# Add and GELU on one core: one 64 KB-row load for the first half of y, another split of the additions, and turns between VectorE and GpSimd

## The chip, the cores and the metric

The kernel runs on one core of a Trainium2 chip. The metric is device time in microseconds (us), the median of several runs; the core also leaves one profiled execution, whose records are read below. The engines that matter are VectorE (DVE in the profile), ScalarE (ACT), GpSimd (POOL) and SyncE (SP), which does no arithmetic and only issues the transfers between the device memory and the on-chip memory (SBUF). TensorE (PE) has no work here.

## The reference

```python
x, y: float32, 1024 x 4096
z = x + y
out = 0.5 * z * (1 + tanh(sqrt(2 / pi) * (z + 0.044715 * z**3)))
```

This is an addition followed by the tanh form of GELU. Each element is read once from x and once from y and written once: 2 x 16.78 MB in, 16.78 MB out.

## The kernel before, in words

Each of the three arrays is seen as 128 partitions x 32768 columns of float32. One SBUF tile `z` holds all 32768 columns: x is loaded into it, y is added in place, the result replaces the sum in place, and the stores read it. The arithmetic goes by 16 chunks of 2048 columns, numbered 0 to 15. For each chunk c there are four steps:

- `add(c)`, line 149: z + y into z, on VectorE for the chunks in the table `by_dve` (line 109), otherwise on GpSimd. Both inputs are in SBUF.
- `mag(c)`, line 154: ScalarE writes |z| into a PSUM buffer `w`. There are two such buffers (`PS = 2`), so `mag(c)` waits for `end(c - 2)` as well as for `add(c)`.
- `gelu(c)`, line 157: ScalarE replaces w by gelu(-w). With a = |z| that is gelu(-a).
- `end(c)`, line 166: VectorE writes max(z, 0) + w into z. One input is in SBUF, the other in PSUM. (For both signs of z, max(z, 0) + gelu(-|z|) is gelu(z).)

All transfers are issued by SP, in one fixed order, on one hardware queue: x0 (columns 0 to 16383, a row of 64 KB in each partition), y0 and y1 (8192 columns each, rows of 32 KB), x1 (columns 16384 to 32767, rows of 64 KB), y2, y3 (8192 columns each), and then the stores s0 (chunks 0 to 7), s1 (chunks 8 to 12) and s2 (chunks 13 to 15). SP takes them strictly in turn: while it waits for one to be allowed, all that follow wait too. The y loads go round two SBUF buffers of 8192 columns (`pool_y`, `bufs=2`, line 115). So y2 needs adds 0 to 3 to be done, since they read the buffer that it overwrites, and y3 needs adds 4 to 7. `begin_early` (line 9) moves the first two loads, which wait for nothing, ahead of the start barrier. `wait_late` (line 23) lets the closing work of the other engines run while the last store is under way.

Each engine's order is written out in lines 173 to 181. The value of an entry of `by_dve` says ahead of which `end` VectorE does that add: `{0: 0, 2: 0, 4: 2, 6: 4, 8: 8, 12: 10}` means adds 0 and 2, end 0, end 1, add 4, end 2, end 3, add 6, end 4, and so on. GpSimd does its ten adds in the order of the chunks, ScalarE `mag` and `gelu` by turns. The table `needs` (line 183) only fixes the order in which the program is written down; the semaphore waits come from which bytes of which tile each instruction reads and writes. One more wait is put in by hand (lines 137 to 143): s0, and with it everything behind it on SP, waits for the first half of `end(8)`, which is why `end(FIRST)` with `FIRST = 8` is cut in two parts.

Of the kernel before, what the change touches and what calls it, by code (L numbers as in the profile page):

```python
# [8 lines left out]
def begin_early(nc, count):  # L9


    head, body = (b.instructions for b in nc.main_func.blocks[:2])
    SP = mybir.EngineType.SP
    moved = [i for i in body if i.engine == SP and isinstance(i, mybir.InstDMACopy)][:count]
    assert not any(i.sync_info and i.sync_info.on_wait for i in moved)
    assert all(i.regs_accessed() == ((), ()) for i in moved)
    at = next(k for k, i in enumerate(head) if i.engine == SP)
    for k, i in enumerate(moved):
        body.remove(i)
        head.insert(at + k, i)  # L20


def wait_late(nc):

    body, end = (b.instructions for b in nc.main_func.blocks[1:3])
    last = [i for i in body if isinstance(i, mybir.InstDMACopy)][-1]
    (sem,) = [u.id for u in last.sync_info.on_update]
    all_done = end[0]  # L30
    reset = next(i for i in end if isinstance(i, mybir.InstDrain) and i.is_reset_sema)
    at = end.index(reset)
    clear = end[at + 1]
    first, stop = reset.reset_range_start, reset.reset_range_stop
    assert all_done.engine == mybir.EngineType.SP and reset.engine == mybir.EngineType.Pool
    assert isinstance(clear, mybir.InstISA) and clear.engine == mybir.EngineType.Pool
    waits = all_done.sync_info.on_wait
    (its,) = [w for w in waits if w.id == sem]

    end[0] = mybir.InstDrain(  # L40
        name=all_done.name, engine=all_done.engine, debug=all_done.debug, is_reset_sema=False,
        sync_info=mybir.SyncInfo(on_wait=[w for w in waits if w.id != sem], on_update=[]),
    )
    parts = []
    for f, e in ((first, sem), (sem + 1, stop)):
        if f < e:
            nc.gpsimd.sem_clear(range(f, e))
            parts.append(nc.cur_bb.bb.instructions.pop())
    end[at + 1 : at + 2] = parts
    end.append(  # L50
        mybir.InstEventSemaphore(
            name=clear.name, engine=mybir.EngineType.Activation, debug=clear.debug,
            sync_info=mybir.SyncInfo(
                on_wait=[its],
                on_update=[
                    mybir.SyncUpdate(
                        sync_type="semaphore", id=sem, ant_name=its.ant_name,
                        update_mode="sem-sub-imm", update_value=its.wait_value,
                    )
                ],  # L60
            ),
        )
    )


@with_exitstack
def kernel(
    ctx: ExitStack,
    tc: tile.TileContext,
    x: bass.AP,  # L70
    y: bass.AP,
    out: bass.AP,
):

    nc = tc.nc
    P = nc.NUM_PARTITIONS
    fp32 = mybir.dt.float32
    act = mybir.ActivationFunctionType
    alu = mybir.AluOpType

    N, D = x.shape
    assert N % P == 0
    TOT = N // P * D  # L90
    xv, yv, ov = (a.rearrange("(p n) d -> p (n d)", p=P) for a in (x, y, out))

    YS = 8192
    CH = 2048
    PS = 2
    xloads = [16384, 16384]
    yloads = [8192, 8192, 8192, 8192]
    FIRST = 8
    stores = [16384, 10240, 6144]

    def ranges(sizes):
        ends = [sum(sizes[: i + 1]) for i in range(len(sizes))]
        assert ends[-1] == TOT
        return [(e - f, e) for e, f in zip(ends, sizes)]

    xr, yr, sr, cr = (ranges(r) for r in (xloads, yloads, stores, [CH] * (TOT // CH)))
    C = len(cr)

    by_dve = {0: 0, 2: 0, 4: 2, 6: 4, 8: 8, 12: 10}

    def over(rs, lo, hi):
        return [i for i, (a, b) in enumerate(rs) if a < hi and b > lo]

    pool_sb = ctx.enter_context(tc.tile_pool(name="xz", bufs=1))
    pool_y = ctx.enter_context(tc.tile_pool(name="y", bufs=2))
    pool_w = ctx.enter_context(
        tc.tile_pool(name="w", bufs=PS, space=bass.MemoryType.PSUM)
    )

    zt = pool_sb.tile([P, TOT], fp32, tag="z", name="z")  # L120
    yt, wt, ends = {}, {}, {}

    def load_x(i):
        a, b = xr[i]
        nc.sync.dma_start(out=zt[:, a:b], in_=xv[:, a:b])  # L125

    def load_y(i):
        a, b = yr[i]
        s, o = divmod(a, YS)
        if o == 0:  # L130
            yt[s] = pool_y.tile([P, YS], fp32, tag="y", name=f"y{s}")
        nc.sync.dma_start(out=yt[s][:, o : o + b - a], in_=yv[:, a:b])

    def store(i):
        a, b = sr[i]
        ins = nc.sync.dma_start(out=ov[:, a:b], in_=zt[:, a:b])
        if i == 0:
            tc.add_manual_dep(
                ins.ins,
                ends[FIRST].name,  # L140
                mybir.DependencyInfo(mybir.DependencyClass.Sync, mybir.DependencyReason.DATA),
                reason="the stores join the queue when the last load is nearly done",
            )

    def add(c):
        a, b = cr[c]
        s, o = divmod(a, YS)
        eng = nc.vector if c in by_dve else nc.gpsimd
        eng.tensor_add(out=zt[:, a:b], in0=zt[:, a:b], in1=yt[s][:, o : o + b - a])  # L149

    def mag(c):
        a, b = cr[c]
        wt[c] = pool_w.tile([P, CH], fp32, tag="w", name=f"w{c}")
        nc.scalar.activation(out=wt[c], in_=zt[:, a:b], func=act.Abs)  # L154

    def gelu(c):
        nc.scalar.activation(  # L157
            out=wt[c], in_=wt[c], func=act.Gelu_apprx_tanh, scale=-1.0
        )

    def end(c):
        a, b = cr[c]
        parts = 2 if c == FIRST else 1
        n = (b - a) // parts
        for o in range(0, b - a, n):
            ins = nc.vector.scalar_tensor_tensor(  # L166
                out=zt[:, a + o : a + o + n], in0=zt[:, a + o : a + o + n], scalar=0.0,
                in1=wt[c][:, o : o + n], op0=alu.max, op1=alu.add,
            )
            ends.setdefault(c, ins.ins)  # L170


    sp = []
    for i, (a, b) in enumerate(xr):
        sp += [(load_x, i)] + [(load_y, j) for j, (c, _) in enumerate(yr) if a <= c < b]
    sp += [(store, i) for i in range(len(stores))]
    pool = [(add, c) for c in range(C) if c not in by_dve]
    dve, acts = [], []
    for c in range(C):
        dve += [(add, k) for k in sorted(by_dve) if by_dve[k] == c] + [(end, c)]  # L180
        acts += [(mag, c), (gelu, c)]

    needs = {
        load_x: lambda i: [],
        load_y: lambda i: [
            (add, c) for c in over(cr, yr[i][0] - 2 * YS, yr[i][1] - 2 * YS)
        ],
        add: lambda c: [(load_x, i) for i in over(xr, *cr[c])]
        + [(load_y, i) for i in over(yr, *cr[c])],
        mag: lambda c: [(add, c)] + ([(end, c - PS)] if c >= PS else []),  # L190
        gelu: lambda c: [(mag, c)],
        end: lambda c: [(gelu, c)],
        store: lambda i: [(end, c) for c in over(cr, *sr[i])] + [(end, FIRST)],
    }
    queues = [sp, pool, acts, dve]
    done = set()
    with tc.manual_schedule():
        one = pool_sb.tile([P, 1], fp32, tag="one", name="one")
        nc.vector.memset(one, 0.0)  # L199
        nc.scalar.activation(out=one, in_=one, func=act.Gelu_apprx_tanh)  # L200
        while any(queues):
            moved = False
            for q in queues:
                while q and all(n in done for n in needs[q[0][0]](q[0][1])):
                    fn, arg = q.pop(0)
                    fn(arg)
                    done.add((fn, arg))
                    moved = True
                    if q is not sp:
                        break  # L210
            assert moved, [q[:1] for q in queues]

    ctx.close()
    tc.close()
    tc.compile()  # L215
    begin_early(nc, 2)
    wait_late(nc)
# [30 lines left out]
```

## Time and profile before

| what | us |
|---|---|
| median of 8 runs | 120.13 (120.03 to 120.29) |
| the profiled execution | 120.08 |
| its span, first to last recorded work | 118.6 |
| DMA engines busy | 98.7% of the span |
| ACT busy, DVE busy, POOL busy | 60.8, 59.8, 55.5 |
| bytes moved | 50.33 MB, 424 GB/s over the span |

The span leaves out 1.5 us around the recorded work. [...] The DMA figure is the mean over 16 DMA engines, which share each transfer: every one moves 8 of its 128 rows. A row is recorded as one packet with a start, a duration and a size. A transfer has landed when the last of the 16 has reported its share. Times in the text are counted from the span's start.

### The profile page before, as it was taken

Reading aid. Unit: us, or ns where it says so; the run is one execution under the profiler, and the core shown is the slowest. Engines: PE = TensorE matmul, PEld = TensorE weight load, DVE = VectorE, ACT = ScalarE, POOL = GpSimd, SP = SyncE. Lnnn points to the kernel's source line nnn. Section 1 sums busy time; section 2 is a strip of 40 time slices with the busy share of each in tenths; the row PEclk is TensorE's granted clock in tenths of the full one; section 3 lists DMA queues with packets and bytes.
Section 4 is the critical chain, followed back from the end, with each engine's and each line's share of the span. In section 5 each row is a group of like instructions: output and inputs, shape, how many; then the busy total and the mean of one; then the engine's idle time right before and its main releaser. Section 6 shows DMA issues by size and latency. Waiting matters only on the chain.

```text
span 118.6 us, 160 instructions
## 1 busy us (share of the span) xinstructions
DVE 59.8 (50%) x24; ACT 60.8 (51%) x34; POOL 55.5 (47%) x14
## 2 busy tenths in 40 slices
DVE  0000000000399999699994584257999457742000
ACT  5000000000057979999379705797798999940000
POOL 0000000000399999998000029999999999200000
DMA  9899888989999988988899998998899889999996
GB/s 354 354 420 641 354 354 354 497 387 464 420 409 475 531 354 354 707 354 354 354 464 420 398 486 354 531 531 354 354 597 464 354 354 442 442 442 442 390 406 265
DMA packets 1296, 50.33 MB, mean 424 GB/s; under 512 B 144, under 2 KB 144, under 8 KB 144
## 3 DMA queue, kind: packets, MB, share of 16 engines
q1 hardware_dynamic: 1296, 50.33, 98.7%
HBM read 33.55 MB, written 16.78 MB: 424 GB/s over the span
## 4 chain that ended last, share of the span: by engine, by line
DMA 48%; POOL 34%; POOLq 4%; ACT 3%; DVE 2%; issue 0%; SPq 0%; DVEq 0%
DMA y<-in_y_dram 48%; POOL z L149 34%; POOLq L215 4%; DVE z L166 2%; ACT w L154 2%; ACT w L157 2%; SPq L125 0%; POOLq L149 0%; DVEq L166 0%
## 5 line engine op out<-in xcount | busy, mean ns | idle before, releaser
L149 POOL TENSOR_TENSOR z<-z,y 128x2048 f32<-128x2048 f32 x10 | 55.3, 5566 | 45.7 <-DMA y<-in_y_dram 45.7
L154 ACT ACTIVATE w<-z 128x2048 f32<-128x2048 f32 x16 | 30.1, 1880 | 42.6 <-DVE z L149 36.1
L166 DVE SCALAR_TENSOR_TENSOR z<-z,w 128x2048 f32<-128x2048 f32 (+1 forms) x17 | 36.4, 2157 | 16.0 <-ACT w L157 16.0
L149 DVE TENSOR_TENSOR z<-z,y 128x2048 f32<-128x2048 f32 x6 | 24.0, 4008 | 30.4 <-DMA y<-in_y_dram 30.4
L157 ACT ACTIVATE w<-w 128x2048 f32<-128x2048 f32 x16 | 29.8, 1862 | 0.5
L200 ACT ACT_TABLE_LOAD x1 | 1.3, 1283 | 1.2 <-PEq L232 1.2
L199 DVE MEMSET one<- 128x1 f32 x1 | 0.1, 59 | 1.3 <-PEq L232 1.3
L200 ACT ACTIVATE one<-one 128x1 f32<-128x1 f32 x1 | 0.2, 203 | 0.0
L232 POOL MEMSET const-float32-0.0<- 128x1 f32 x1 | 0.1, 98 | 0.2 <-issue 0.2
L232 POOL MEMSET const-bfloat16-1.0<- 128x1 bf16 x1 | 0.1, 102 | 0.0
L232 POOL MEMSET const-uint8-127<- 128x1 uint8 x1 | 0.1, 102 | 0.0
L232 POOL MEMSET const-float32-1.0<- 128x1 f32 x1 | 0.1, 99 | 0.0
## 6 DMA issues: line engine op xcount, KB each, us to landing
y<-in_y_dram SPq DMA_DIRECT2D x4, 4096.0 KB, 28.2
out_dram<-z SPq DMA_DIRECT2D x1, 5120.0 KB, 14.9
out_dram<-z SPq DMA_DIRECT2D x1, 3072.0 KB, 10.9
z<-in_x_dram SPq DMA_DIRECT2D x2, 40.3
out_dram<-z SPq DMA_DIRECT2D x1, 21.6
```

The lines of the kernel that those rows point to most:

```text
L149: eng.tensor_add(out=zt[:, a:b], in0=zt[:, a:b], in1=yt[s][:, o : o + b - a])
L154: nc.scalar.activation(out=wt[c], in_=zt[:, a:b], func=act.Abs)
L157: nc.scalar.activation(out=wt[c], in_=wt[c], func=act.Gelu_apprx_tanh, scale=-1.0)
L166: ins = nc.vector.scalar_tensor_tensor(out=zt[:, a + o : a + o + n], in0=zt[:, a + o : a + o + n], scalar=0.0, in1=wt[c][:, o : o + n], op ...
L199: nc.vector.memset(one, 0.0)
L200: nc.scalar.activation(out=one, in_=one, func=act.Gelu_apprx_tanh)
L215: tc.compile()
L232: nc = _bacc.Bacc("TRN2", target_bir_lowering=False, num_devices=1)
```

## The change

The first half of y becomes one load of 16384 columns (rows of 64 KB) into one buffer `y` of that size, in place of two loads into two buffers of half the size; the SBUF taken is the same. The second half of y is still two loads of 8192 columns, y1 and y2 in the new numbering, into the first and the second half of that buffer. VectorE does adds 0, 1, 3, 5, 7, 8, 11 and 14 and GpSimd the other eight. Six of GpSimd's adds (2, 4, 6, 9, 12, 15) get a wait for the VectorE add just before them, by the table `turn`; adds 10 and 13 have none. The hand-made wait of the stores is taken out, and with it the cut of `end(8)` in two.

```diff
-    YS = 8192
+    YS = 16384
-    yloads = [8192, 8192, 8192, 8192]
-    FIRST = 8
+    yloads = [16384, 8192, 8192]
-    by_dve = {0: 0, 2: 0, 4: 2, 6: 4, 8: 8, 12: 10}
+    by_dve = {0: 0, 1: 0, 3: 1, 5: 3, 7: 5, 8: 6, 11: 9, 14: 12}
+
+    turn = {2: 1, 4: 3, 6: 5, 9: 8, 12: 11, 15: 14}
-    pool_y = ctx.enter_context(tc.tile_pool(name="y", bufs=2))
+    yt = pool_sb.tile([P, YS], fp32, tag="y", name="y")
     def load_y(i):
         a, b = yr[i]
-        s, o = divmod(a, YS)
-        if o == 0:
-            yt[s] = pool_y.tile([P, YS], fp32, tag="y", name=f"y{s}")
-        nc.sync.dma_start(out=yt[s][:, o : o + b - a], in_=yv[:, a:b])
+        o = a % YS
+        nc.sync.dma_start(out=yt[:, o : o + b - a], in_=yv[:, a:b])
     def store(i):
         a, b = sr[i]
-        ins = nc.sync.dma_start(out=ov[:, a:b], in_=zt[:, a:b])
-        if i == 0:
+        nc.sync.dma_start(out=ov[:, a:b], in_=zt[:, a:b])
+
+    def add(c):
+        a, b = cr[c]
+        o = a % YS
+        eng = nc.vector if c in by_dve else nc.gpsimd
+        ins = eng.tensor_add(
+            out=zt[:, a:b], in0=zt[:, a:b], in1=yt[:, o : o + b - a]
+        )
+        adds[c] = ins.ins
+        if c in turn:
             tc.add_manual_dep(
                 ins.ins,
-                ends[FIRST].name,
+                adds[turn[c]].name,
                 mybir.DependencyInfo(mybir.DependencyClass.Sync, mybir.DependencyReason.DATA),
-                reason="the stores join the queue when the last load is nearly done",
+                reason="the two engines take turns on their shared port",
             )
     def end(c):
         a, b = cr[c]
-        parts = 2 if c == FIRST else 1
-        n = (b - a) // parts
-        for o in range(0, b - a, n):
-            ins = nc.vector.scalar_tensor_tensor(
-                out=zt[:, a + o : a + o + n], in0=zt[:, a + o : a + o + n], scalar=0.0,
-                in1=wt[c][:, o : o + n], op0=alu.max, op1=alu.add,
-            )
-            ends.setdefault(c, ins.ins)
+        nc.vector.scalar_tensor_tensor(
+            out=zt[:, a:b], in0=zt[:, a:b], scalar=0.0, in1=wt[c],
+            op0=alu.max, op1=alu.add,
+        )
```

`needs` is changed to match: a y load needs the adds that read the part of the buffer that it overwrites, an add in `turn` needs its predecessor, and a store needs only its own chunks' `end`.

## The prediction

> **What bounds the kernel now.** I first read the page's slices and DMA queue.
>
> ```profile
> DMA  9899888989999988988899998998899889999996
> ...
> q1 hardware_dynamic: 1296, 50.33, 98.7%
> ```
>
> The sixteen DMA engines have no slice without work, and 98.7% of the span is packet time. No compute engine passes 51%. Then the chain that ended last:
>
> ```profile
> DMA 48%; POOL 34%; POOLq 4%; ACT 3%; DVE 2%; issue 0%; SPq 0%; DVEq 0%
> ```
>
> It says "POOL 34%", which looks like a second bound. It isn't: the chain ends at the last store's issue, and asks only what released that issue. Whether the issue mattered is seen from what was still in the queue. So I read SP's issues in the timeline, beside the transfers:
>
> ```profile
> 44.74 13.57 SPq L132 DMA_DIRECT2D y<-in_y_dram  x2
> ...
> 77.68 30.30 SPq L136 DMA_DIRECT2D out_dram<-z  x3
> ```
>
> With the answers for single lines: y2 issued at 44.74 and y3 at 57.98, s0 at 77.68, s1 at 96.42, s2 at 107.65. From issue to landing they take 25.4, 21.9, 21.6, 14.9 and 10.9 us, so the landings are x0 21.7, y0 31.4, y1 41.2, x1 60.4, y2 70.2, y3 79.9, s0 99.3, s1 111.3, s2 118.6. Each transfer is issued before the one ahead of it has landed. The packet records say the same more finely: the first of the 16 engines takes up y2 at 59.58, y3 at 69.28, s0 at 78.98, s1 at 98.30 and s2 at 110.39, each about 0.5 us before the last engine is through with its predecessor. No engine has a hole between two transfers. So the time is the sum of the packets: a 65536-byte packet takes 2418 ns (median), one of 32768 bytes 1213 ns; the 8 packets of one engine make 19.35 us for a half of x and 9.70 for a y load.
>
> How late may a transfer be issued? s0 was issued at 77.68 and taken up without a hole at 78.98, so 1.30 us ahead is enough. The very first load was issued at 0.00 and its first packet began at 1.00, so an empty queue answers in 1.00 us. The lead needed lies in 1.00 to 1.30.
>
> Last, the durations that decide when transfers are released:
>
> ```profile
> L149 POOL TENSOR_TENSOR z<-z,y 128x2048 f32<-128x2048 f32 x10 | 55.3, 5566 | 45.7 <-DMA y<-in_y_dram 45.7
> L154 ACT ACTIVATE w<-z 128x2048 f32<-128x2048 f32 x16 | 30.1, 1880 | 42.6 <-DVE z L149 36.1
> L166 DVE SCALAR_TENSOR_TENSOR z<-z,w 128x2048 f32<-128x2048 f32 (+1 forms) x17 | 36.4, 2157 | 16.0 <-ACT w L157 16.0
> L149 DVE TENSOR_TENSOR z<-z,y 128x2048 f32<-128x2048 f32 x6 | 24.0, 4008 | 30.4 <-DMA y<-in_y_dram 30.4
> L157 ACT ACTIVATE w<-w 128x2048 f32<-128x2048 f32 x16 | 29.8, 1862 | 0.5
> ```
>
> ```profile
> L149 POOL TENSOR_TENSOR z<-z,y x10: 4511/5558/6629, 31.6 to 96.9; 128x2048 f32<-128x2048 f32 x10
> L149 DVE TENSOR_TENSOR z<-z,y x6: 2279/3640/6594, 31.5 to 83.1; 128x2048 f32<-128x2048 f32 x6
> ```
>
> The reader sees in the last two (minimum/median/maximum) that an undisturbed add takes 4.51 us on POOL and 2.28 on DVE, and up to 6.6 where one waits for the other. The single instructions show how: DVE's add 0 ends at 33.81, POOL's add 1, started at 31.56, ends 4.36 later at 38.17, DVE's add 2, started at 33.72, ends 2.15 later at 40.32. They never overlap. `end` on DVE takes 2.27 to 2.29 beside a running POOL add.
>
> [...]
>
> **The change part by part.**
>
> *Row size.* Each engine swaps 16 packets of 1213 ns (19.41 us) for 8 of 2418 (19.34): 0.064 us less, and one report packet (9 ns) fewer: **-0.07 us**. x1, the same shape at the same place in the stream, shows 2418. That the larger rows cost anything is excluded by x0 and x1 unless y's memory differs from x's; bounds -0.10 to 0. All later run-outs are moved 0.07 forward.
>
> *The first add comes later.* It waits for the whole half, at 41.1 where y0 had landed at 31.4: 9.7 us. What hides this is that DMA has x1 queued, which keeps it busy to 59.5. Without that cover the whole 9.7 would show. What is late next is ScalarE, then the releases of y1, y2, s0, s1, s2. I therefore chain all steps through with the durations above (DVE to ACT wake 0.03, ACT to DVE 0.03 where DVE made the sum and 0.10 where POOL did, back-to-back DVE instructions 0.08 overlapped, `mag` + `gelu` 3.69 when ScalarE is never idle). The same rules on the order of before give s0, s1 and s2 within 0.04 us of the trace.
>
> One price isn't in the trace: POOL waiting for a DVE semaphore. ACT wakes 0.03 after DVE; POOL started its first add 0.14 after y0 landed. I take 0.04 and 0.15 as the ends, the middle as the value; nothing excludes more. Behind a waiting POOL add only POOL's later adds are queued, with `mag`, `gelu`, `end` of those chunks and so SP's stores.
>
> *First half.* add 0 41.2-43.5, add 1 to 45.7, POOL add 2 45.8-50.3; end 0 at 47.3-49.6; add 3 starts at 49.5, is held up until 50.3, ends at 52.4. **y1 released at 52.4 to 52.5**; x1 is taken off the queue until 59.5, so 7.0 us early. Then POOL add 4 to 57.0, ends 1 and 2 to 57.0, add 5 to 59.3, add 6 to 63.9, ends 3 and 4 to 64.5, add 7 to 66.7. **y2 released at 66.7 to 66.8**; y1 runs out at 69.2: 2.4 early (before: 11.3). y1 lands at 70.1: add 8 to 72.5, end 6 to 74.7, end 7 to 76.9. **s0 released at 76.9**; y2 runs out at 78.9: 2.0 early. Removing the hand-made wait is thus worth nothing by itself: s0 was 1.3 early before, and joins 0.8 us sooner.
>
> *Second half.* add 8 (DVE) to 72.5, add 9 (POOL) to 77.0-77.15, add 10 to 81.5-81.6. DVE's add 11, started at 80.7, is held up until then and ends at 83.7-83.8. POOL add 12 waits its turn: to 88.2-88.4; add 13 to 92.7-92.9. add 14, started at 91.9, is held up and ends at 94.85-95.1. `gelu(12)` was done at 93.4, but end 12 is queued behind add 14 on DVE: 94.8 to 97.05-97.3. **s1 released at 97.1 to 97.3**; s0 runs out at 98.2: 0.9 to 1.15 early, where 1.00 to 1.30 is needed. This is the one edge. Taking 97.2 and the 1.00 of the first load, s1 begins at 98.2: **0.00**. Both ends: nothing (97.1 + 1.00), or 97.3 + 1.30 - 98.2 = 0.4 us lost. ends 13, 14, 15 end at 99.5, 103.3, 107.0. **s2 released at 107.0**, 3.3 early (before 2.7). POOL's add 15 ends at 99.6, early by more than 1 us for its `mag` at 100.8.
>
> *Turns, fewer GpSimd adds, `end(8)` whole.* Two chunks move from 4.5 us on POOL to 2.3 on DVE[...]. All this goes into the releases above, and DMA hides it; without that cover the end of the last chunk, 107.0 against 107.6, would be worth -0.6.
>
> *Issue.* One transfer fewer saves 0.33 us of SP time at 1.26, when x0 has 20 us to go: nothing.
>
> Sum for the profiled execution: 120.08 - 0.07 + 0.00 = 120.01. The median of the runs is 0.05 higher, so 120.13 - 0.07 = **120.06**. A change of 0.2% (0.24 us) is about the least that the scatter of these runs, 120.03 to 120.29, lets one tell from none.
>
> **The rivals.**
>
> *A, DMA stays full: 120.06* (own range 119.95 to 120.3, with a hole of up to 0.3 before s1). For it: every release but one has 2 us or more. Chance 0.77.
>
> *B, slower: s1 is late.* Place: the chain y1 landing, add 8, 9, 10, 11, 12, 13, 14, end 12. Mechanism: the waits of POOL in the two turns on it (adds 9 and 12) take longer than 0.15. Each 0.1 more delays s1 by 0.2. From a release at 97.2 (lead 1.00) each 0.1 us of delay costs 0.1; from 97.5 the total is beyond +0.24. A wake-up of 0.35 gives s1 at 97.7, a hole of 0.5 and 120.13 - 0.07 + 0.5 = 120.55. For it: the margin is nil, and a queue that has run dry may restart slowly (the first packet of each engine took 3.03 us instead of 2.42). Against: no wait in the trace is that slow. Chance 0.14.
>
> *C, the single y buffer is tracked as a whole.* Then y1 would wait for adds 4 to 7 as well, to 66.7 instead of 52.4, and DMA would be empty from 59.5 to 67.7: 120.06 + 8.2 = 128.3. Against: `z` is one tile too, and x1 was issued into its second half at 1.63 and s0 read its first half while adds wrote the second. Chance 0.04.
>
> *D, faster: the compute chain did count.* If the releases govern, as "POOL 34%" suggests, s2's 0.6 us is gained: 120.13 - 0.6 = 119.5. Against: s1 ran until 110.88, 3.2 us after s2's issue. Chance 0.05.
>
> *E, ScalarE becomes the bound.* It starts 9.7 us later, and 16 x 3.69 = 59 us from 43.5 is 102.5. Even with its idle 2 us it has done at 104.6, and s2 would have to slip by 2.3 us before it costs. That is 120.06 again, inside A.
>
> **How the numbers follow.** Same: A, 0.77. Slower: B and C, 0.18. Faster: D, 0.05. The range 119.9 to 120.55 takes in A and the nearer part of B; C, D and B's far part, about 0.15, stay outside.
>
> **What would show it.** DMA share 98.5% or more, packets 1152. Right: first adds at 41.2, y1 issued near 52.4, y2 near 66.7, s0 near 76.9, s1 at 97.1 to 97.3, s2 near 107; undisturbed durations for all turned POOL adds, hold-ups only for adds 3, 11, 14. Wrong: y1 issued near 67 (C); s1 after 97.5 with a slice of lower DMA share near 98 (B); packets of the new y load other than 2418 ns.

## The result, and the profile after

The changed kernel takes 120.74 us (median of 12 runs, 120.22 to 120.98), the kernel before 120.21 (33 runs, 120.03 to 120.87): a ratio of 1.0039, 95% interval 1.0029 to 1.005 (this ratio and all that follow compare the means of the runs, so they can differ a little from a ratio of medians). The forecast was 120.06, no difference, in a range of 119.9 to 120.55. The profiled execution took 120.52, with a span of 119.0 against 118.6.

From the page of the changed kernel, the slices and the queue:

```profile
DMA  9899888988899889988898998998899889999896
...
q1 hardware_dynamic: 1152, 50.33, 98.5%
```

The transfers still bound the kernel, with fewer packets (1152 instead of 1296) and no visible hole. The chain that ended last, same page:

```profile
DMA 49%; DVE 18%; ACT 15%; issue 8%; SPq 0%; DVEq 0%
```

POOL's 34% have gone from the chain, and the time has not gone with them: as the prediction read it, that share never set the end. The adds, from the answer for line 142 (count, minimum/median/maximum in ns, first and last start in us):

```profile
L142 DVE TENSOR_TENSOR z<-z,y x8: 2283/2292/2992, 41.2 to 92.2; 128x2048 f32<-128x2048 f32 x8
L142 POOL TENSOR_TENSOR z<-z,y x8: 4520/4532/4539, 45.7 to 95.3; 128x2048 f32<-128x2048 f32 x8
```

The turns work: no POOL add is held up (4539 ns at most, where the longest of before took 6629), and three DVE adds only by 0.6 to 0.7 us (2992 at most). Held up means that the add ends only after the other engine's: adds 3, 11 and 14 end 2.14 to 2.15 us after the POOL add ahead of them (52.41 after 50.26, 83.97 after 81.82, 95.20 after 93.06). That the two engines share a port, as the `reason` in the code has it, no run here shows. SP's issues, from the timeline:

```profile
52.49 14.60 SPq L132 DMA_DIRECT2D y<-in_y_dram  x2
...
77.16 30.48 SPq L136 DMA_DIRECT2D out_dram<-z  x3
```

The second of the y loads by itself:

```profile
66.77 0.33 SPq L132 DMA_DIRECT2D y<-in_y_dram  x1
```

The y loads are issued at 52.49 and 66.77, s0 at 77.16, s1 at 97.43, s2 at 107.31; forecast were 52.4 to 52.5, 66.7 to 66.8, 76.9, 97.1 to 97.3 and 107.0. So the engines do what was worked out, and the extra time is in the transfers themselves. The packet records show where. Given is when the last engine is through with a transfer, in us from the span's start:

| | x, y up to x1 | next y load | last y load | s0 | s1 | s2 |
|---|---|---|---|---|---|---|
| before | 60.05 | 69.75 | 79.46 | 98.79 | 110.88 | 118.15 |
| changed | 60.09 | 70.02 | 79.98 | 99.30 | 111.39 | 118.67 |
| later by | 0.04 | 0.27 | 0.52 | 0.51 | 0.51 | 0.52 |

All the loss arises in the last two loads, 0.23 and 0.25 us each. Four packets of the load ahead of the last, started from 68.2, and 13 of the last one, started from 69.4 to 69.9, took more than 100 ns over the usual 1213, up to 1754. With the ends of the one load and the starts of the next matched in order, no engine was without a packet for more than 0.06 us there. DMA did not run dry; the reads became slower around the point where the last load, issued at 66.77, took over.

### The profile page after: what moved, and what is told of

Same layout as the page of the kernel before. It is cut to its first block, busy times and chain, and to the rows that moved or that the text cites. A ratio compares the mean times of both kernels' runs of the same rounds, so it can differ in the third digit from the quotient of the medians.

```text
span 119.0 us, 158 instructions
## 1 busy us (share of the span) xinstructions
DVE 55.9 (47%) x25; ACT 60.4 (51%) x34; POOL 36.3 (31%) x12
## 2 busy tenths in 40 slices
DMA packets 1152, 50.33 MB, mean 423 GB/s; under 512 B 128, under 2 KB 128, under 8 KB 128
## 3 DMA queue, kind: packets, MB, share of 16 engines
q1 hardware_dynamic: 1152, 50.33, 98.5%
## 4 chain that ended last, share of the span: by engine, by line
DMA 49%; DVE 18%; ACT 15%; issue 8%; SPq 0%; DVEq 0%
DMA y<-in_y_dram 49%; DVE z L166 12%; ACT w L157 8%; DVE z L142 7%; ACT w L160 7%; SPq L127 0%; DVEq L166 0%; DVEq L142 0%; SPq L132 0%
## 5 line engine op out<-in xcount | busy, mean ns | idle before, releaser
L142 POOL TENSOR_TENSOR z<-z,y 128x2048 f32<-128x2048 f32 x8 | 36.1, 4530 | 63.3 <-DVE z L142 63.3
L166 DVE SCALAR_TENSOR_TENSOR z<-z,w 128x2048 f32<-128x2048 f32 x16 | 36.5, 2284 | 8.8 <-ACT w L160 8.6
L142 DVE TENSOR_TENSOR z<-z,y 128x2048 f32<-128x2048 f32 x8 | 20.2, 2541 | 41.3 <-DMA y<-in_y_dram 41.3
```

The lines of the kernel that those rows point to most:

```text
L142: ins = eng.tensor_add(out=zt[:, a:b], in0=zt[:, a:b], in1=yt[:, o : o + b - a])
L166: nc.vector.scalar_tensor_tensor(out=zt[:, a:b], in0=zt[:, a:b], scalar=0.0, in1=wt[c], op0=alu.max, op1=alu.add,)
```

## The experiments

Theories at the start. *Late issue*: a load that joins the queue a few us before it is needed is read with stretched packets. *Row size*: the 64 KB rows of y disturb later reads. *Order*: the new split of the adds and the turns do. "Lead" below is the time from the issue of a transfer by SP to its first packet, both from the profile; it was 11.3 us for the last load before and 2.7 in the changed kernel. Each ratio is to the kernel before on the same chip; the runs were spread over three chips, which the table at the end of this section calls A, B and C.

**Only the issue of the last load is made late, in the kernel before.**

```diff
-        nc.sync.dma_start(out=yt[s][:, o : o + b - a], in_=yv[:, a:b])
+        ins = nc.sync.dma_start(out=yt[s][:, o : o + b - a], in_=yv[:, a:b])
+        if i == 3:
+            tc.add_manual_dep(ins.ins, ends[6].name, ...)
```

> The kernel before, with one more wait: y3 is issued only when end 6 is done, at about 66.3 instead of 58.0, 3.0 us before the first engine runs out of y2 at 69.28 (in the changed kernel the last load was issued 2.7 us before its first packet). Nothing else moves. Late-issue theory (a load that joins the queue shortly before it is needed has its first packets stretched, as its own last predecessor's are): packets at 68 to 72 of 1400 to 1700 ns instead of 1213, +0.25 to +0.5 us, ratio to before 1.002 to 1.004. Row-size theory (the 64 KB load of the first half of y shifts the phase of the 16 engines against each other[...]) and order theory (the new split of the additions and their turns disturb the loads): 1.000.

Measured: 120.33, ratio 1.0014 (1.0006 to 1.0022), less than the 1.002 to 1.004 that the theory had expected. The issue of y3, from the timeline:

```profile
66.54 0.33 SPq L132 DMA_DIRECT2D y<-in_y_dram  x1
```

In the profiled execution y3 had packets of up to 395 ns over, one engine stood for 0.54 us and began only at 70.49, and y3 was done 10.37 us after y2 instead of 9.71. (That execution, 120.87, is the slowest of its runs; the median shows less.) A late issue alone is enough for part of the loss, with rows, split and order as before.

**The changed kernel with its last load cut in two.**

```diff
-    yloads = [16384, 8192, 8192]
+    yloads = [16384, 8192, 4096, 4096]
```

> The changed kernel, with its last load cut in two of 4096 columns: the first part needs adds 4 and 5 alone and is issued at about 59.3, ten us before it is taken up at 69.4; the second at 66.8, some 7 us before it is taken up at 74.3. One transfer more costs under 0.05 us. Late-issue theory: no stretched packets around 68 to 72, ratio to before 1.000 to 1.001. Row-size theory and order theory: as the changed kernel, 1.004.

Measured: 120.24, ratio 1.0001 (0.9988 to 1.0015). SP's timeline has the two last y loads, at 59.37 and 66.84, and s0:

```profile
59.37 7.80 SPq L132 DMA_DIRECT2D y<-in_y_dram  x2
77.03 0.35 SPq L136 DMA_DIRECT2D out_dram<-z  x1
```

No packet around 68 to 72 was stretched. The second part was issued at the same time as the changed kernel's last load, and its first packet came at 74.2. So neither the 64 KB rows nor the adds' order cost anything here, nor does the moment 66.8. This points to how far ahead of the need the issue lies, though the rows of the last load are shorter here, too.

**The first half of y in two loads, first with the early adds that follow from it, then with the first add held until both have landed.**

```diff
-    yloads = [16384, 8192, 8192]
+    yloads = [8192, 8192, 8192, 8192]
```

and in the second case also, in `add`:

```diff
+        if c == 0:
+            tc.add_manual_dep(ins.ins, loads[1].name, ...)
```

> The changed kernel, with the first half of y in two loads of 8192 columns again (still one buffer): the adds begin at 31.4, y2 and y3 are issued about 9 us earlier, at about 43 and 57. Late-issue theory: no stretch, 1.000. Row-size theory: 1.000. Order theory: 1.004.

> The changed kernel, with the first half of y in two loads of 8192 columns, but the first add waits for both, so that the adds begin at 41.2 and the last load is issued at 66.8 as in the changed kernel. Only the row size is undone. Late-issue theory: 1.004 as the changed kernel, with stretched packets at 68 to 72. Row-size theory: 1.000. Order theory: 1.004.

Measured: 1.0 within the interval for the first (0.9999, 0.9989 to 1.001), 1.0019 (1.0005 to 1.0033) for the second, with the last load issued 2.3 us ahead. In the first of them, y3 had rows of 32 KB as in the changed kernel and a lead of 12.2 us. The order theory falls: all adds in the new order, with their turns, cost nothing. Lateness without the large row costs again, but less than the changed kernel's 1.0039.

**Is that difference real, and does a smaller lead cost more?** The changed kernel and the last kernel again, side by side, and two more leads in the kernel before:

```diff
-                ends[6].name,
+                gelus[7].name,
```

for a lead of 1.7, and `ends[5].name` for 6.5.

> The changed kernel itself, beside the next run on the same chip: does the stretch of packets at 68 to 72 come back at the same place, and does its row size add to what the late issue costs? Late-issue theory alone: the same ratio as the next run, 1.002 to 1.004. Late issue plus row size: 1.004, above the next run by 0.002.

> The changed kernel with the first half of y in two loads and the first add held until both have landed, once more, beside the changed kernel. Late-issue theory alone: equal to it. Late issue plus row size: 1.002.

> The kernel before, y3 issued after gelu 7, at about 67.7, 1.6 us before the first engine runs out of y2, where it was 2.7 in the run that waited for end 6 (1.0014) and 11.3 in the kernel before. Late-issue theory: the loss grows as the lead falls, so more than 1.0014, and packets stretched after 69; the first packets of s0, which was taken up without a stretch with a lead of 1.3, say that stores need less, so this must be a load's own need. Rival: 1.30 us is enough for a load too, and what the run with end 6 lost is due to where in the stream the wait fell: 1.000 to 1.001.

> The kernel before, y3 issued after end 5, at about 62.4, 6.9 us before the first engine runs out of y2. Late-issue theory: that is enough, no stretch, 1.000, since y1 in the changed kernel was issued 7.0 us ahead and its own first packets took 1213 ns. Rival (every added wait ahead of a load costs something, however early): 1.001.

Measured: 1.0037 (1.0024 to 1.0051) and 1.0018 (1.0007 to 1.0029), then 1.0001 (0.9992 to 1.001) and 0.9995 (0.9987 to 1.0003). The values of the first pair came back, though their intervals overlap. The loss is not the same in every execution: those of the kernel with two loads lie between 120.20 and 121.03, those of the kernel before with a lead of 1.7, on the same chip, between 120.11 and 120.53. So one profile can miss it. (The profiled execution of the changed kernel was its fastest, 120.31; it has no packet of the last two loads over by 100 ns, and up to 0.15 us without one at the hand-over.) The third result breaks the late-issue theory as I had put it: issued at 67.78 instead of 66.54, *later* than in the first experiment, the load cost nothing. Its issue, from the timeline:

```profile
67.78 0.33 SPq L132 DMA_DIRECT2D y<-in_y_dram  x1
```

The new theory was that only a stretch of lead costs. It says something that no "later is worse" can say: holding the changed kernel's last load back still further must make it faster.

**The changed kernel, last load held back further; and leads of 2.0, 3.5 and 5.2 in the kernel before.** In the first, `load_y` of the changed kernel:

```diff
+        if i == 2:
+            tc.add_manual_dep(ins.ins, mags[6].name, ...)
```

In the others the wait of y3 in the kernel before is for a fill of a spare tile of 768 columns put behind end 6 on VectorE, for mag 7, and for gelu 6:

```diff
+        if c == 6:
+            ends[c] = nc.vector.memset(pause, 0.0).ins
...
+                mags[7].name,
...
+                gelus[6].name,
```

> The changed kernel, with one more wait ahead of its last load: y2 is issued after mag 6, at about 67.7, where it was 66.8, so its lead falls from 2.7 to 1.7 us. Phase theory (a load loses when its issue falls into a certain stretch before it is needed, about 2.2 to 2.8 us, and not when it comes later, as the run with a lead of 1.6 showed): the ratio falls to 1.000 to 1.001, so waiting longer makes it faster. Plain late-issue theory (less lead, more loss): 1.004 or more. Row-size theory (the larger row costs by itself once the load is late): 1.002 to 1.004.

> The kernel before, with a fill of 768 columns of a spare tile on VectorE after end 6, and y3 issued after it, at about 67.2, 2.1 us before the first engine runs out of y2: between the run with 2.7 (1.0014) and the one with 1.6 (1.0001). Phase theory: 1.0005 to 1.003, it lies at the lower edge of the stretch in which issuing costs. Plain late-issue theory: at least 1.0014. That the run with 2.7 was chance: 1.000.

> The kernel before, y3 issued after mag 7, at about 65.8, 3.5 us before the first engine runs out of y2. Phase theory: if the costly stretch is one packet long (1.2 us, from 2.8 to about 1.7), 1.000; if it begins earlier, 1.001 to 1.002. Plain late-issue theory: between 1.000 and 1.0014.

> The kernel before, y3 issued after gelu 6, at about 64.0, 5.3 us before the first engine runs out of y2. All theories 1.000 to 1.0005; a loss here would say that the costly stretch comes back with each packet.

Measured: 1.0000 (0.9984 to 1.0016), 1.0000 (0.9992 to 1.0008), 1.0004 (0.9995 to 1.0012), 1.0003 (0.9994 to 1.0012). At the lead of 2.0 the new theory had expected 1.0005 to 1.003. The changed kernel with its last load issued 0.75 us later is at 120.20, no slower than before; the changed kernel itself was not run on this chip. In its timeline, against 52.49 and 66.77, the two loads are at 52.41 and 67.52:

```profile
52.41 15.43 SPq L132 DMA_DIRECT2D y<-in_y_dram  x2
```

The windows of 3 us around the point of the hand-over, of the changed kernel (columns: window, length, busy time of DVE, ACT, POOL with counts, clock, DMA share, GB/s; a packet counts in the window in which it starts):

```profile
69.00:72.00 3.00, 1.55 (x1) 2.97 (x3) 0.00 (x0) 1.00 0.90 350
```

and the same with the load held back:

```profile
69.00:72.00 3.00, 1.84 (x1) 2.97 (x3) 0.00 (x0) 1.00 1.07 459
```

ScalarE and GpSimd do the same in both and VectorE nearly so; fewer packets start in the first. Nothing here says that the compute engines slow the reads.

**Is it a fixed time, or a place among the packets?** The empty queue answered 1.00 us after the first load's issue. By an estimate from that and from the packets of 1.21 us, with a lead of 2.3 to 3.0 the new rows would come with 1.3 to 2.0 us of packets still ahead, while an engine is at its last packet but one. Shorter packets ahead tell these apart:

```diff
-    yloads = [16384, 8192, 8192]
+    yloads = [16384, 4096, 4096, 8192]
```

once as it is, once with the last load held for mag 6.

> The changed kernel, with the load ahead of the last one cut in two of 4096 columns, so that the packets ahead of the last load take about 0.61 us instead of 1.21. The last load is issued at 66.8 as in the changed kernel, 2.3 to 2.7 us before its first packet. Packet theory (the costly moment is that in which an engine is at the last packet but one of its queue when the new rows arrive, about 1.0 us after the issue): they now arrive with two to three packets ahead, so 1.000 to 1.001. Time theory (a lead of 2.3 to 3.0 us costs, whatever the packets): 1.004 as the changed kernel.

> The same, with the last load held until mag 6 as in the run that brought the changed kernel back to 1.000: issued at about 67.6, 1.7 to 1.9 us before its first packet. Packet theory: the rows arrive 0.7 to 0.9 us before an engine runs out, which is now its last packet but one (0.61 to 1.21), so it loses, 1.001 to 1.004. Time theory: outside 2.3 to 3.0, so 1.000.

Measured: 1.0087 (1.0064 to 1.0111) and 1.0068 (1.0051 to 1.0085), more than either theory allows. These two runs decide nothing on the question, as more than the packets had changed: adds 8 and 9 could begin earlier, and s0 was issued at 75.53 and 75.71, 4.0 and 3.8 us ahead of its first packet. In both, the last load's own later packets were stretched, most of all the seventh of each engine's eight in the first run (started from 76.8), by up to 892 ns, and the eighth in the second (from 78.0), by up to 1061. That pointed to the first store, which the kernel before holds back by hand.

**The same with the store held back too; and the store alone, in the kernel before.** In the first two s0 waits for gelu 8:

```diff
+        if i == 0:
+            tc.add_manual_dep(ins.ins, gelus[8].name, ...)
```

In the third the hand-made wait of the kernel before is taken out, in the fourth it is for `mags[FIRST]` instead of `ends[FIRST]`:

```diff
-        if i == 0:
-            tc.add_manual_dep(ins.ins, ends[FIRST].name, ...)
```

> The run with short rows ahead of the last load (1.0087), whose first store had moved to 75.5, four us before its first packet, and whose last load was stretched at 76.6 to 79.5: now the store waits for gelu 8 too and is issued at about 77.2, a lead of 2.1 to 2.4 as in the changed kernel. The last load keeps its lead of 2.6 to 2.8. Packet theory: 1.000 to 1.001. Time theory: 1.002 to 1.004. If the early store was not the cause of that run's loss: 1.009.

> The same with the last load held until mag 6, 1.6 to 1.9 us before its first packet (1.0068 with the store at 75.7). Packet theory: 1.001 to 1.004. Time theory: 1.000. If the early store was not the cause: 1.007.

> The kernel before, without the hand-made wait of s0 for end 8 (the cut of end 8 in two stays): s0 is issued at about 70.0, right after end 7, nine us before its first packet. The prediction held that this wait is worth nothing by itself: 1.000. If a store that joins while many load packets are still ahead disturbs them: slower, 1.003 to 1.01, with the stretch in packets of y3 that start a us or more after 70.

> The kernel before, s0 waiting for mag 8 in place of end 8: issued at about 74.6, 4.4 us before its first packet, as in the two runs with short rows. If the early store is what stretched the last load there: 1.004 to 1.008, with stretched packets of y3 from 76 on. If it was the short rows: 1.000.

Measured: 1.0028 (1.0016 to 1.004), 1.0004 (0.9991 to 1.0017), 1.0069 (1.0056 to 1.0082), 1.0071 (1.0059 to 1.0084). Holding the store back takes away the larger part of both losses, 1.0087 to 1.0028 and 1.0068 to 1.0004, with the two pairs on different chips. What is left in the first pair speaks for the fixed time: with packets of half the length ahead, a lead of 2.5 still costs and one of 1.8 still doesn't. The second pair shows a second effect, of the other kind of transfer. Without the hand-made wait s0 is issued at 70.11:

```profile
70.11 0.35 SPq L136 DMA_DIRECT2D out_dram<-z  x1
```

and y3, issued at 58.06, lands after

```profile
DMA to landing us min/median/max: 22.8/22.8/22.8
```

where in the kernel before, issued at 57.98, it took

```profile
DMA to landing us min/median/max: 21.9/21.9/21.9
```

Sixteen packets of y3, started from 76.6 to 77.1, took some 830 ns more than usual in the mean: the seventh of the eight of every engine. With s0 waiting for mag 8 its issue is

```profile
74.66 0.35 SPq L136 DMA_DIRECT2D out_dram<-z  x1
```

and the stretched packets are the same sevenths, from 76.6, by 700 ns in the mean. So in these runs a store that has long been queued behind a load slows the load's last rows, from some 3.4 us before its own first packet (80.0 in both, where it came at 79.0 in the kernel before). That the two issues lie 4.6 us apart did not move the place.

The leads of the last load together, up to 6.5 us and without the runs in which the store disturbed the load, in the order of the lead. The issue and the first packet are those of the profiled execution (the chip of the first run of the changed kernel is not on record):

| kernel | chip | issued | first packet | lead | ratio | interval |
|---|---|---|---|---|---|---|
| before, after gelu 7 | A | 67.78 | 69.44 | 1.7 | 1.0001 | 0.9992 to 1.001 |
| changed, after mag 6 | B | 67.52 | 69.26 | 1.7 | 1.0000 | 0.9984 to 1.0016 |
| short rows ahead, after mag 6, s0 held | C | 67.69 | 69.45 | 1.8 | 1.0004 | 0.9991 to 1.0017 |
| before, after end 6 and a fill | B | 67.41 | 69.39 | 2.0 | 1.0000 | 0.9992 to 1.0008 |
| changed, two loads, first add late | A | 67.08 | 69.41 | 2.3 | 1.0019 | 1.0005 to 1.0033 |
| short rows ahead, s0 held | C | 66.93 | 69.44 | 2.5 | 1.0028 | 1.0016 to 1.004 |
| changed, two loads, again | A | 66.88 | 69.45 | 2.6 | 1.0018 | 1.0007 to 1.0029 |
| changed, again | A | 66.96 | 69.53 | 2.6 | 1.0037 | 1.0024 to 1.0051 |
| changed | - | 66.77 | 69.45 | 2.7 | 1.0039 | 1.0029 to 1.005 |
| before, after end 6 | A | 66.54 | 69.51 | 3.0 | 1.0014 | 1.0006 to 1.0022 |
| before, after mag 7 | B | 65.86 | 69.33 | 3.5 | 1.0004 | 0.9995 to 1.0012 |
| before, after gelu 6 | B | 64.14 | 69.33 | 5.2 | 1.0003 | 0.9994 to 1.0012 |
| before, after end 5 | A | 62.77 | 69.24 | 6.5 | 0.9995 | 0.9987 to 1.0003 |

Every lead from 2.3 to 3.0 that was tried costs in the mean, none outside does that a run can tell. On chip A 1.7 and 6.5 are free and 2.3 to 3.0 cost; on chip C 1.8 is free and 2.5 costs. So that a smaller lead is free again shows within a single chip, on A and on C. Where the stretch ends, between 2.0 and 2.3 and between 3.0 and 3.5, compares A with B, on which no lead within the stretch was run without an early store.

One rival is only half excluded. In all the costly runs the last load was released by an instruction of VectorE, in most of the free ones by one of ScalarE. The free runs at 2.0 and 6.5 were released by VectorE as well; the first of them is on chip B.

## Why the prediction was wrong

**What bounds the kernel: right.** The transfers did before and do after; POOL left the chain and gained nothing.

**Row size, -0.07: the sign right, the size half.** Done with x0, the engines needed 19.326 us for y's first half in the changed kernel and 19.362 before: 0.04 us less. The sum had added the durations of the packets, but in the trace of before packets of 32 KB follow each other every 1209 ns and not every 1213, those of 64 KB every 2414 and not every 2418; sixteen such overlaps of 4 ns instead of eight took half of the gain. A 64 KB row showed no cost by itself: the changed kernel with the last load cut in two, or held back, has the same row and no loss that a run can tell (1.0001 and 1.0000).

**The first add comes later, and the chain of releases: right** for y1 and y2 to 0.1 us; s0, s1 and s2 came 0.2 to 0.3 later than worked out, as the load that they follow had landed 0.3 later. The price that the trace of before did not show, POOL waking after DVE, was 0.08 us (add 1 ended at 45.66, add 2 began at 45.74), within 0.04 to 0.15.

**"How late may a transfer be issued?" is the step that failed.** It took 1.30 us from a store and 1.00 from the first load into an empty queue, and held that any lead over these is free. So y2's release, "2.4 early", was waved through, though the same line showed that the change cuts its lead from 11.3. The runs showed in its place that for a load behind a load a lead of 2.3 to 3.0 us costs 0.14 to 0.4%, while at 1.7, 2.0, and 3.5 or more no loss can be told. No slower wait and no hole entered into it: rival B's place, s1, was issued at 97.43 and its first packet came at 98.67, with no engine standing. (That edge was eased by the loss itself, which had put off s0's end; in the changed kernel with the last load held back, without that loss, the lead of s1 was 1.18 and again no engine stood.) The prediction's one edge was watched, and the loss came from a place that it had called safe. None of its signs of being wrong appeared, since none looked at the packets of y2. Rival A's picture, no hole, came true, and the time was outside A's range all the same. The sum has no term for y2, its 0.00 is that of s1; in the profiled execution the term should have been about +0.5 us.

**The hand-made wait, "worth nothing by itself": right in the changed kernel by its new timing alone, wrong as a statement.** In the changed kernel end 7 comes at 77.1 and s0 has a lead of 2.2 us without the wait, and no packet of y2 that started after 70 is stretched by 100 ns. In the kernel before, taking it out costs 0.69%. The working asked only whether a store can be issued too late.

**The other rivals.** C is refuted (y1 at 52.49, not 67). D is refuted: s2 was issued 0.34 us earlier than before and the end came later. E is as worked out: ScalarE ended at 104.9, hidden.

**What stays open.** Why reads slow down in this band of lead, and why a queued store slows the loads ahead of it, isn't settled: no run here looks at the mechanism. In the runs of the table the first packet always comes at 69.2 to 69.5, so there a lead and a moment of issue are the same thing; only the run with the last load cut in two tells them apart. The changed kernel lost twice as much, 1.0039 and 1.0037, as its relative with two smaller loads, 1.0019 and 1.0018. Since the larger row alone showed no cost (1.0001 with the last load in two, 1.0000 with it held back), it may only shift the lead within the band; no run separates the two. Whether a load of another size than 4 MiB has the same band was not tried, nor was a store behind a load with a lead between 2.2 and 3.8 us.

## What to carry to other kernels

When a change moves the issue of a transfer closer to its need, a lead that was enough for one kind of transfer need not be enough for another: here 1.30 us was enough for a store behind a load, and 2.3 to 3.0 cost a load behind a load 0.14 to 0.4%. So compare load behind load with load behind load. In a kernel bound by transfers, look at the durations of single packets at each hand-over as well as for holes, since a stream without holes can still be slower (here no engine was without a packet for more than 0.06 us, and the last load was through 0.52 us later); and look at more than one execution, since not every one shows the loss (the one of 120.31 us had no packet of the last two loads over by 100 ns). And try the issue later as well as earlier: here, with 0.75 us of further delay, no loss could be told any more (1.0000).

## What the runs showed of the hardware that was not expected

- In these runs a load of 32 KB rows behind another load, on one queue, loses 0.14 to 0.4% of 120 us in the mean of its executions when it is issued 2.3 to 3.0 us ahead of its first packet: single packets take up to 1754 ns instead of 1213 in the changed kernel (1832 with short rows ahead), or one engine begins 0.3 to 0.5 us late. At 1.7, 2.0 and 3.5 us the ratios are 1.0001, 1.0000 and 1.0004.
- In these runs a store queued behind a load 5.3 or 9.9 us ahead of its own first packet stretches the last packet but one of the load on each of the 16 engines, by 700 and 830 ns in the mean, and costs 0.7% (1.0071 and 1.0069 in the kernel before). With leads of 1.3 (before) and 2.2 (changed) it doesn't: the load's packets took 1221 ns at most in the former, and in the latter none that started after 70 was over by 100 ns.
- A store behind a store didn't mind a lead of 2.7 (s2 before): its predecessor's packets stayed at 1514 ns (1536 at most).
